# High parts of all k first, then low parts, in the weight-stationary matmuls of a two-layer float32 decoder

## The chip, the cores and the metric

One core of one Trainium2 chip. The metric is the device time of one execution in microseconds (us), as the median of several runs; shorter is better.

## What is computed

A decoder of two layers on 256 tokens of 1024 features, all in float32. Layer 0 is an mLSTM mixer, layer 1 an attention whose only block is the causal one of 256 tokens (so its block selection has no effect); each is followed by a ConvFFN. The keys and values of layer 1 are made from the residual stream after layer 0.

```
for l in range(2):
    h = h + mixer_l(rmsnorm(h))             # projections of 1024 features, w_out or w_o at the end
    u = rmsnorm(h) @ w_up                   # 1024 -> 2 x 2816
    c = conv_b + causal convolution of u over 3 tokens, by feature
    val, gate = split(c)
    h = h + (silu(gate) * val) @ w_down     # 2816 -> 1024
```

## The kernel before

**Precision.** TensorE multiplies in float32r. Each float32 operand is split into a high part (rounded to float32r) and a low part (the rest), and a product is summed from three passes: high by high, high by low and low by high. ScalarE (ACT) makes the high part of a weight unit and VectorE (DVE) the low part (`unit`, L163, the copies at L171 and L172, in two pieces). An activation is split in the same way (`split`, L175), in the ConvFFN by ACT (L339) and POOL (L340).

**Two ways of multiplying.** Most matmuls hold the weights still: a tile of 128 output features by 256 tokens is summed in one PSUM bank over all k, where k counts blocks of 128 input features. For each k, `steps_w` (L226) issues two matmuls: the high weights against the high and low parts of the activation side by side (512 columns, L241), and the low weights against the high part (256 columns, L245). The high weights times the low activation thus gather in the second half of the bank; `whole` (L278) or `residual` (L288) adds the halves. Where `apart` is false (the last tile of the kernel alone), both products of the high weights go to the first half, as two matmuls of 256 columns (L239). The v, o, and attention projections hold the activation still instead (`steps_x`, L254, three matmuls of 512 columns per k at L262 to L264).

**The order before.** The high matmul goes first for k = 0, as it opens the bank. For every later k the low one goes first, then the high one. So a tile of eight k runs high, low, low, high, low, high, and so on, and where one tile follows another, two highs meet.

**Stages.** Keys and queries of the mLSTM (`kq_steps`, eight column tiles, the first two mixed k by k with the gates' matmuls), v and o, the output projection `project_out` (L297: four column tiles over k = 0 to 3, the same four over k = 4 to 7, then four more), the up projection of the ConvFFN (`pair`, L353: 22 pairs of tiles, value and gate, the first `AHEAD` = 2 pairs k by k as the operands come), the convolution of each pair (`conv`, L319, `finish`, L333), and the down projection (`down`, L372: eight column tiles over 22 k, with two weight units of 11 k each). Down's first steps go: k = 0 to 18 of tile 0, k = 0 to 10 of tile 1, then the rest of both, so that the last convolutions have time to end. The attention layer then runs in the same pattern.

The first `DEFER` = 3 pairs of an up stage multiply an operand that lacks 1/rms; `rescale` (L342) makes the operands once more with 1/rms in them (L348 on DVE, L350 on ACT, L351 on POOL), and the pairs from 3 on use these. 1/rms comes from `Rstd` (L206): `sums` (two small matmuls at L212, then L214 on DVE and a power on POOL at L216) and `row` (transposes at L221, a copy at L223).

**What sets the order of work.** TensorE runs in the order in which the program emits its instructions. `mix` (L68) emits a list of steps, each with an assumed cost in us, and slips in other items once the summed cost reaches an item's time; a step costs 0.32. The instructions of DVE, ACT and POOL are ordered by the framework, with a simulated timeline of the program. SyncE issues the loads. Weight units pass through three raw buffers and four buffers each for the high and the low parts; five PSUM banks hold the tiles (`acc`), three more serve the rest (`mis`).

Of the kernel before, what the change touches and what calls it, by code (L numbers as in the profile page):

```python
# [42 lines left out]
# columns of the per-partition parameter array  # L43
# [5 lines left out]
# columns of the array that is needed first: the gates' weights, the first gain  # L49
# [6 lines left out]
class Once:  # L56
    """A thing that is made when it is first asked for."""
# [10 lines left out]
def mix(steps, items=()):  # L68
    """Emit the steps, each a (cost, function), and the items, each a (time, function), among them."""
    items, now = list(items), 0.0  # L70
    for cost, step in steps:
        while items and items[0][0] <= now:
            items.pop(0)[1]()
        step()
        now += cost
    for _, item in items:
        item()
# [3 lines left out]
def yoco_kernel(ctx: ExitStack, tc: tile.TileContext, A, out):  # L81
    nc = tc.nc
    # the tensor engine works in the order of this program
# [10 lines left out]
    # ---- the residual stream, transposed: hT[:, k] holds features k*128.. by tokens  # L94
# [3 lines left out]
    # rows on every partition: the gates' biases, the gains of k's and q's first 32 features  # L98
# [19 lines left out]
    # the gates' weights: for each k the high parts, the low parts, and zeros  # L118
# [3 lines left out]
    # while the first loads run: the tensor engine's clock rises, the activation tables are loaded  # L122
# [8 lines left out]
    # ---- constants made on the chip  # L131
    ident = const.tile([P, P], F32, name="ident")
    make_identity(nc, ident)
    # adds rows m and m + 8
    both8 = const.tile([4 * MH, 2 * MH], F32, name="both8")
    nc.gpsimd.tensor_tensor(out=both8, in0=ident[:4 * MH, :2 * MH], in1=ident[:4 * MH, 2 * MH:4 * MH], op=OP.add)
    # sel[:, h] has ones in row h alone
# [4 lines left out]
    # [s, t], 1 where s <= t, else 0; columns 128.. are ones  # L142
# [4 lines left out]
    # mLSTM: [s, t], 0 where s <= t, else BIG; columns 128.. are free  # L147
# [6 lines left out]
    # attention: [t, s], columns 128.. 0 where s <= t, else -BIG; the columns before are free  # L154
# [7 lines left out]
    # ---- weights: a unit is loaded whole and split exactly into two float32r parts  # L162
# [20 lines left out]
    # ---- RMSNorm: the gain goes into the matmul's operand, 1/rms is applied to its result  # L183
    # an operand: for each k its high part, its low part, and both side by side
# [21 lines left out]
    class Rstd:  # L206
        """1/rms of the residual stream: a column over the tokens and a row on every partition."""
# [17 lines left out]
    # ---- matmuls: three exact passes of hi and lo parts  # L225
    def steps_w(ps, w, at, x, ks, kall, done=None, apart=True):  # L226
        """ps[n, tokens] += W[k, n].T x[k, tokens]; at(k) gives the columns of k in w. The high parts of W
        times the low parts of x may be summed apart, in the second half of ps."""
        xh, xl, both = x

        def one(k):
            (hi, lo), p = w(), ps()
            c = slice(at(k), at(k) + P)
            last = k == kall - 1

            def high():
                if not apart:
                    for n, xs in enumerate((xh, xl)):
                        nc.tensor.matmul(p[:, :S], hi[:, c], xs[k], start=k == 0 and n == 0, stop=last and n == 1)  # L239
                    return  # L240
                nc.tensor.matmul(p, hi[:, c], both[k], start=k == 0, stop=last)  # L241

            if k == 0:
                high()
            nc.tensor.matmul(p[:, :S], lo[:, c], xh[k], start=False, stop=False)  # L245
            if k > 0:
                high()
            if last and done is not None:
                done(p)

        return [(0.32, lambda k=k: one(k)) for k in ks]

    def steps_x(t, units, x, done):
        """ps[tokens, 512] = x[k, tokens].T W[k, 512] over two units of four k."""  # L254
# [15 lines left out]
    def block_x(src, first, x, done):  # L270
        """Both token tiles of 512 columns: units first and first + 1 of src."""
# [522 lines left out]
```

## Time and profile before

| | |
|---|---|
| median of three runs | 608.62 us (608.0 to 608.84) |
| profiled execution: span from first to last instruction | 607.1 us |
| TensorE matmul busy | 593.5 us |
| TensorE weight loads busy | 505.9 us |
| VectorE busy | 495.6 us |
| ScalarE (ACT) busy | 393.2 us |
| POOL busy | 171.8 us |

The profile gives only the span of its own execution; the median of the runs lies 1.5 us above it. Busy times of different engines overlap. Matmul records overlap as well, since a matmul's record goes on after the next has started, so the distance from start to start tells the rate. A few matmul records are missing. In the trace `xa` and `xb` are two sets of projection operands, `f` is the activation of a ConvFFN, `hi` and `lo` the parts of the weights, `acc` a PSUM bank of a tile and `mis` one of the other banks.

### The profile page before, as it was taken

The numbers are of one execution on the slowest core, as the hardware profiler recorded it, in microseconds if no ns is written. First come the engines' busy times: TensorE is split into PE (matmuls) and PEld (weight loads), VectorE is DVE, ScalarE is ACT, GpSimd is POOL, SyncE is SP. The second block draws the span as 40 slices with busy tenths as digits, with TensorE's granted clock in tenths as the row PEclk, the third lists the DMA queues.
The fourth block names the chain that finished last, engine by engine and source line by source line (L and its number), as shares of the span: only waits on it lengthen the run. The fifth ranks groups of instructions, "written<-read, shape, count | busy, mean of one in ns | idle before, by whom it ended". The sixth has DMA issues, their size and how long they took to land.

```text
span 607.1 us, 8990 instructions
## 1 busy us (share of the span) xinstructions
PE 593.5 (98%) x3278; PEld 505.9 (83%) x3278; DVE 495.6 (82%) x837; ACT 393.2 (65%) x713; POOL 171.8 (28%) x186
## 2 busy tenths in 40 slices
PE   7899999999999999899999999999999999998997
PEld 4787888888888888788888878888888888887887
DVE  7897667989999999967768786467999999998550
ACT  5756776667886777755556687554878767675330
POOL 6600310352545344211111100022445453441000
PEclk8999999999999999899999999999999999999999
DMA  6874333526444543465754533335353445336530
GB/s 243 317 264 169 139 138 140 208 84 263 159 179 166 191 165 133 161 207 184 266 203 181 198 123 143 125 135 208 132 215 140 185 172 198 138 131 229 212 108 18
DMA packets 18621, 105.79 MB, mean 174 GB/s; under 512 B 2320, under 2 KB 3856, under 8 KB 9104
## 3 DMA queue, kind: packets, MB, share of 16 engines
q1 hardware_dynamic: 18576, 105.21, 47.0%
q8 instruction: 26, 0.43, 0.3%
q14 instruction: 19, 0.16, 0.1%
HBM read 104.15 MB, written 1.05 MB: 173 GB/s over the span
## 4 chain that ended last, share of the span: by engine, by line
PE 48%; DVE 37%; issue 8%; ACT 3%; POOL 2%; DMA 1%; SPq 0%; POOLq 0%; DVEq 0%; ACTq 0%
PE acc L241 15%; DVE y L329 15%; DVE lo L172 14%; PE acc L245 8%; PE acc L262 6%; PE acc L264 6%; PE acc L263 6%; DVE whole L282 4%; DVE xs L348 1%; ACT y L326 1%; DVE xa L181 1%; PE acc L239 1%; ACT hi L171 1%; DMA hT<-xT 1%; PE mis L547 1%
## 5 line engine op out<-in xcount | busy, mean ns | idle before, releaser
L172 DVE TENSOR_TENSOR lo<-raw,hi 128x1024 fp32r<-128x1024 f32 (+2 forms) x218 | 248.6, 1168 | 30.5 <-ACT hi L171 30.2
L241 PE MATMUL acc<-xb,hi 128*128 128x512 f32 x736 | 252.3, 396 | 0.6 <-POOL xb L351 0.6
L171 ACT ACTIVATE hi<-raw 128x1024 fp32r<-128x1024 f32 (+2 forms) x218 | 199.9, 964 | 61.3 <-PE acc L241 29.5
L245 PE MATMUL acc<-xb,lo 128*128 128x256 f32 x736 | 191.2, 279 | 0.0
L241 PEld LDWEIGHTS acc<-xb,hi 128*128 128x128 f32 x736 | 131.8, 188 | 26.3 <-POOL xb L351 1.3
L245 PEld LDWEIGHTS acc<-xb,lo 128*128 128x128 f32 x736 | 138.7, 188 | 8.0
L241 PE MATMUL acc<-f,hi 128*128 128x512 f32 x330 | 116.6, 398 | 1.0 <-POOL f L340 1.0
L329 DVE SCALAR_TENSOR_TENSOR y<-whole,par,y 128x254 f32<-128x254 f32 (+1 forms) x176 | 110.0, 644 | 3.2 <-ACT y L326 2.8
L245 PE MATMUL acc<-f,lo 128*128 128x256 f32 x352 | 97.5, 284 | 3.0 <-ACT f L339 3.0
L338 POOL TENSOR_TENSOR a<-sg,y 128x256 f32<-128x256 f32 x44 | 57.8, 1314 | 98.4 <-ACT sg L336 98.4
L241 PEld LDWEIGHTS acc<-f,hi 128*128 128x128 f32 x330 | 61.8, 190 | 14.5 <-POOL f L340 1.4
L245 PEld LDWEIGHTS acc<-f,lo 128*128 128x128 f32 x352 | 66.8, 190 | 5.0 <-ACT f L339 3.6
L326 ACT ACTIVATE y<-whole,par 128x256 f32<-128x256 f32 x88 | 51.7, 594 | 20.8 <-DVE whole L282 18.8
L241 PE MATMUL acc<-xa,hi 128*128 128x512 f32 x160 | 57.5, 401 | 0.7 <-DVE hT L291 0.5
L262 PE MATMUL acc<-hi,xa 128*128 128x512 f32 x128 | 53.4, 417 | 0.0
L340 POOL TENSOR_TENSOR f<-a,f 128x256 fp32r<-128x256 f32 x44 | 42.3, 962 | 36.6 <-ACT f L339 36.6
L264 PE MATMUL acc<-hi,xa 128*128 128x512 f32 x128 | 50.1, 391 | 0.0
L199 POOL TENSOR_TENSOR sqacc<-sqacc,sq 128x256 f32<-128x256 f32 x18 | 16.3, 908 | 119.0 <-ACT sq L198 119.0
L263 PE MATMUL acc<-lo,xa 128*128 128x512 f32 x128 | 50.0, 391 | 0.0
L245 PE MATMUL acc<-xa,lo 128*128 128x256 f32 x160 | 44.4, 289 | 0.8 <-DVE lo L172 0.7
L282 DVE TENSOR_TENSOR whole<-acc,whole 128x256 f32<-128x256 f32 (+1 forms) x97 | 39.4, 412 | 0.0
L281 ACT ACTIVATE whole<-acc 128x256 f32<-128x256 f32 (+1 forms) x97 | 35.4, 368 | 6.0 <-PE acc L241 5.8
(180 smaller groups left out, 637.7 us busy)
## 6 DMA issues: line engine op xcount, KB each, us to landing
raw<-w_up SPq DMA_DIRECT2D x44, 1024.0 KB, 4.8
raw<-w_down SPq DMA_DIRECT2D x32, 704.0 KB, 4.0
raw<-w_kqv SPq DMA_DIRECT2D x12, 1024.0 KB, 4.8
raw<-w_vo SPq DMA_DIRECT2D x8, 1024.0 KB, 4.8
raw<-w_out SPq DMA_DIRECT2D x4, 1024.0 KB, 4.8
raw<-w_o SPq DMA_DIRECT2D x4, 1024.0 KB, 4.8
raw<-w_kq SPq DMA_DIRECT2D x2, 1024.0 KB, 7.8
raw<-w_kq SPq DMA_DIRECT2D x4, 256.0 KB, 5.5
```

What stands on the lines that cost most here:

```text
L171: nc.scalar.activation(hi[:, c], raw[:, c], AF.Copy)
L172: nc.vector.tensor_tensor(lo[:, c], raw[:, c], hi[:, c].bitcast(F32), OP.subtract)
L241: nc.tensor.matmul(p, hi[:, c], both[k], start=k == 0, stop=last)
L245: nc.tensor.matmul(p[:, :S], lo[:, c], xh[k], start=False, stop=False)
L262: nc.tensor.matmul(p, xh[k][:, ts], hi[:, c], start=k == 0, stop=False)
L263: nc.tensor.matmul(p, xh[k][:, ts], lo[:, c], start=False, stop=False)
L264: nc.tensor.matmul(p, xl[k][:, ts], hi[:, c], start=False, stop=k == KD - 1)
L282: nc.vector.tensor_tensor(y, ps[:rows, :S], y, OP.add)
L326: nc.scalar.activation(y, u, AF.Identity, bias=b, scale=w[2])
L329: nc.vector.scalar_tensor_tensor(y[:, d:], u[:, :S - d], w[j], y[:, d:], op0=OP.mult, op1=OP.add)
L338: nc.gpsimd.tensor_tensor(out=a, in0=sg, in1=y[0], op=OP.mult)
L340: nc.gpsimd.tensor_tensor(out=al[i], in0=a, in1=ah[i].bitcast(F32), op=OP.subtract)
```

## The change

`steps_w` no longer issues one step per k with two matmuls. It returns all high matmuls of the k that it is given (0.22 us each), and then all low ones (0.11 us each). The first high still opens the bank; the last low now closes it and calls `done`. Callers that passed all k of a tile get high times eight, then low times eight. `down` calls it once per weight unit, so 11 highs are followed by 11 lows. Callers that pass one k at a time (the first two pairs of an up stage, the first two tiles of keys and queries) get high, then low, for each k. `kq_steps` takes the k as an argument for that. Comments and docstrings are taken out as well.

```diff
     def steps_w(ps, w, at, x, ks, kall, done=None, apart=True):
...
         xh, xl, both = x
 
-        def one(k):
-            (hi, lo), p = w(), ps()
+        ks = list(ks)
+
+        def high(k):
+            (hi, _), p = w(), ps()
             c = slice(at(k), at(k) + P)
+            if apart:
+                nc.tensor.matmul(p, hi[:, c], both[k], start=k == 0, stop=False)
+            else:
+                for n, xs in enumerate((xh, xl)):
+                    nc.tensor.matmul(p[:, :S], hi[:, c], xs[k], start=k == 0 and n == 0, stop=False)
+
+        def low(k):
+            (_, lo), p = w(), ps()
             last = k == kall - 1
-
-            def high():
-                if not apart:
-                    for n, xs in enumerate((xh, xl)):
-                        nc.tensor.matmul(p[:, :S], hi[:, c], xs[k], start=k == 0 and n == 0, stop=last and n == 1)
-                    return
-                nc.tensor.matmul(p, hi[:, c], both[k], start=k == 0, stop=last)
-
-            if k == 0:
-                high()
-            nc.tensor.matmul(p[:, :S], lo[:, c], xh[k], start=False, stop=False)
-            if k > 0:
-                high()
+            nc.tensor.matmul(p[:, :S], lo[:, at(k):at(k) + P], xh[k], start=False, stop=last)
             if last and done is not None:
                 done(p)
 
-        return [(0.32, lambda k=k: one(k)) for k in ks]
+        return [(0.22, lambda k=k: high(k)) for k in ks] + [(0.11, lambda k=k: low(k)) for k in ks]
...
             def down(n, ks):
                 apart = gains is not None or n < KD - 1
-                return [s for k in ks for s in
-                        steps_w(pd[n], wd[2 * n + k // 11], lambda q: (q % 11) * P, act, [k], KF,
+                return [s for u in range(2) for s in
+                        steps_w(pd[n], wd[2 * n + u], lambda q: (q % 11) * P, act,
+                                [k for k in ks if k // 11 == u], KF,
                                 lambda p: residual(n, p, gains, apart), apart)]
...
-        def kq_steps(j):
-            return steps_w(pk[j], wk[j // 2], lambda k: k * 256 + (j % 2) * P, setA, range(KD), KD,
+        def kq_steps(j, ks=range(KD)):
+            return steps_w(pk[j], wk[j // 2], lambda k: k * 256 + (j % 2) * P, setA, ks, KD,
                            (lambda p: kq_done(j)) if j > 2 else None)
...
-        s0, s1 = kq_steps(0), kq_steps(1)
-        mix([s for k in range(KD) for s in (sg[k], s0[k], s1[k])])
+        mix([s for k in range(KD) for s in [sg[k]] + kq_steps(0, [k]) + kq_steps(1, [k])])
```

## Rows read from the trace of the kernel before

**Rows 1.** The page's line of engines: busy us, share of the span, instructions.

```profile
PE 593.5 (98%) x3278; PEld 505.9 (83%) x3278; DVE 495.6 (82%) x837; ACT 393.2 (65%) x713; POOL 171.8 (28%) x186
```

**Rows 2.** Chain of waits by line: 262 to 305, 17 to 37, 150 to 262 us.

```profile
by line: PE acc L241 66.1%; PE acc L245 34.1%
...
by line: PE acc L241 38.4%; PE acc L245 19.8%; POOL tab L607 17.8%; POOL sq L394 8.2%; POOL tab L603 5.1%; issue 3.6%; POOL rc L216 3.4%; PE mis L221 2.2%; PE mis L437 1.1%; PE mis L438 1.1%; PE mis L436 0.6%
...
by line: DVE y L329 37.0%; DVE lo L172 26.3%; issue 14.8%; DVE whole L282 8.3%; PE acc L241 4.7%; ACT y L326 2.7%; PE acc L245 2.0%; ACT hi L171 1.5%; ACT sg L336 1.1%; POOL f L340 0.7%; POOL a L338 0.7%; ACT whole L281 0.5%; ACTq L336 0.0%
```

**Rows 3.** A stretch of up: busy us (xinstructions) of PE, PEld, DVE, ACT, POOL; clock.

```profile
150.00:190.00 40.00, 40.00 (x231) 34.81 (x230) 40.00 (x61) 30.90 (x62) 21.24 (x17) 1.00 0.43 169
```

**Rows 4.** The low matmuls of L245 in a stretch of down: matmuls, then weight loads.

```profile
262.00:302.00 40.00, 31.40 (x115) 21.42 (x114) 1.00 0.59 209
```

**Rows 5.** Timeline (start us, us, group): a 512-column run (35 steps), a 256-column run (42).

```profile
313.98 0.39 PE L262 MATMUL acc<-hi,xa 128*128 128x512 f32 x1
...
321.91 0.39 PE L264 MATMUL acc<-hi,xa 128*128 128x512 f32 x1
...
597.99 0.40 PE L239 MATMUL acc<-f,hi 128*128 128x256 f32 x2
...
603.03 0.40 PE L239 MATMUL acc<-f,hi 128*128 128x256 f32 x2
```

**Rows 6.** Timeline where two tiles of up meet (x2 merges two matmuls).

```profile
151.31 0.63 PE L241 MATMUL acc<-xb,hi 128*128 128x512 f32 x2
151.78 0.39 PE L245 MATMUL acc<-xb,lo 128*128 128x256 f32 x2
152.01 0.40 PE L241 MATMUL acc<-xb,hi 128*128 128x512 f32 x1
```

**Rows 7.** Timeline of layer 0 from the first down matmul to the last activation.

```profile
241.04 0.39 PE L241 MATMUL acc<-f,hi 128*128 128x512 f32 x1
...
248.34 0.41 DVE L282 TENSOR_TENSOR whole<-acc,whole 128x256 f32<-128x256 f32 x1
...
251.73 2.22 DVE L172 TENSOR_TENSOR lo<-raw,hi 128x704 fp32r<-128x704 f32 x2
...
252.00 0.39 PE L241 MATMUL acc<-f,hi 128*128 128x512 f32 x1
...
253.70 0.39 PE L245 MATMUL acc<-f,lo 128*128 128x256 f32 x1 [1.31 <-ACT f L339]
...
254.59 0.80 PE L241 MATMUL acc<-f,hi 128*128 128x512 f32 x1 [0.50 <-POOL f L340]
```

**Rows 8.** The same two waits in layer 1.

```profile
552.10 0.38 PE L245 MATMUL acc<-f,lo 128*128 128x256 f32 x1 [1.67 <-ACT f L339]
...
552.98 0.50 PE L241 MATMUL acc<-f,hi 128*128 128x512 f32 x1 [0.51 <-POOL f L340]
```

**Rows 9.** Stretches right behind these waits, columns as in rows 3 (clock: third last).

```profile
254.30:257.80 3.50, 3.21 (x10) 2.73 (x11) 3.30 (x6) 2.96 (x6) 0.23 (x1) 0.52 0.69 232
...
554.40:557.80 3.40, 3.40 (x21) 3.01 (x20) 2.77 (x5) 1.02 (x2) 0.00 (x0) 1.00 0.94 331
```

**Rows 10.** Timeline of the first up tile with rescaled operands: first high, eighth high.

```profile
134.19 0.40 PE L241 MATMUL acc<-xb,hi 128*128 128x512 f32 x1
...
137.21 0.73 PE L241 MATMUL acc<-xb,hi 128*128 128x512 f32 x2 [0.32 <-POOL xb L351]
```

**Rows 11.** Timeline of keys and queries: the power on POOL, the row's transposes.

```profile
23.64 0.71 POOL L216 TENSOR_TENSOR rc<-ms,mhalf 128x2 f32<-128x2 f32 x1
...
24.41 0.43 PE L221 MATMUL mis<-ident,rc 128*128 128x128 f32 x2 [0.63 <-POOL rc L216]
```

**Rows 12.** Timeline of the first output projection: last operand, its high matmul.

```profile
99.89 0.48 DVE L181 SCALAR_TENSOR_TENSOR xb<-mis,par,xb 128x256 fp32r<-128x256 f32 x1 [0.54 <-ACT xb L180]
...
100.42 0.50 PE L241 MATMUL acc<-xb,hi 128*128 128x512 f32 x1
```

**Rows 13.** Timeline of VectorE: its first rescaled operands in layer 0.

```profile
125.38 0.88 DVE L348 SCALAR_TENSOR_TENSOR xs<-hT,par,rB 128x256 f32<-128x256 f32 x2 [2.33 <-ACT rB L223]
```

## The prediction

> **What bounds the kernel now.** I read the page's engine line first, then the chain of waits by stretch, then start times of single matmuls. TensorE is busy for nearly the whole span [rows 1], but matmul records overlap, so that alone proves nothing. The chain, cut by stretch, does [rows 2]. From 262 to 305 us (down projection of layer 0) it consists of TensorE's own matmuls and nothing else. From 17 to 37 us (keys and queries) it is TensorE, after a piece on POOL. From 150 to 262 us (up projection and the start of down) it is VectorE: the convolution, the low parts of the weights, the sums of the halves; TensorE has 7%. VectorE is there 40.00 of 40 us busy [rows 3]; TensorE never waits either, it only runs ahead. The proof comes at the end: the last up matmul is followed by the first down one at 241.0 us, while VectorE forms the sum of the last up tile at 248.34 us [rows 7], and TensorE then waits for the last activation. So a faster or slower TensorE matters in the down stages, in keys and queries and in the two output projections; in the up stages it mostly changes the wait that follows them.
>
> Counting tiles times k in the code: the up stages have 2 x 22 x 2 x 8 = 704 pairs of a high (512 columns) and a low matmul (256). On TensorE's path are 3 x 64 = 192 pairs outside the ConvFFN and 330 in down (the last tile's 22 steps have three matmuls of 256 and stay as they are in cost); 64 of these run before the wait for the last activation and are covered. That leaves about 460 pairs.
>
> **Rate of the matmuls.** The edit adds and removes no matmul, load or byte on TensorE; it changes which size follows which. A pair takes 40.00/114 = 351 ns in down [rows 4]; I use 350. Grouped runs of 8 or 11 are not in the trace, so I bound them from the nearest rows. A long run of 512 columns with new weights each time takes (321.91 - 313.98)/35 = 227 ns, and a long run of 256 columns (603.03 - 597.99)/42 = 120 ns [rows 5]; both together 347, or 3 ns less per pair. Where two tiles meet, the present order already has two highs and then two lows in a row: 0.47/2 = 235 and 0.23/2 = 115 ns, in sum 350 [rows 6]. The best mixture, 227 + 115, is 8 ns less, the worst, 235 + 120, 5 ns more: -3.7 to +2.3 us over 460 pairs. The new runs begin like the border and go on like the long runs, so I take the middle of the two observed sums, -2 ns a pair: **-0.9 us**.
>
> The trace shows no waiting of a low matmul on its weights: lows in a run keep 115 to 120 ns. The Trainium skill (TensorE: Matmul & The Clock Gate, section Back-to-back issue gap) gives a warm matmul its columns over 2.4 GHz plus 2.5 ns whatever precedes it, thus 325 ns for a pair in either order, by which this term would be nil; the rows show 25 ns more than that, and in both kinds of run, so the measurement decides.
>
> **Wait for the last activation, twice.** Now down runs 19 k of column tile 0, 11 k of tile 1, then k = 19 to 21 of tile 0, alternating. The high of k = 20 goes at 252.00, the low of 21 waits until 253.70 for the high part of the activation, the high of 21 until 254.59 for the low part that POOL makes [rows 7]; layer 1 does the same at 552.10 and 552.98 [rows 8]. After the change the three highs come first, and the high of 21 needs both parts. It still starts at about 254.6, as its operand comes from VectorE and POOL, but the lows of 19, 20 and 21 (3 x 0.12 us) then stand behind it instead of ahead: 0.35 us per layer, **+0.7 us**. Ends: 0, if the activation arrives as early as TensorE does; +0.7.
>
> That wait has a second price. Behind it in layer 0 the granted clock falls: 10 matmuls in 3.5 us at 0.52, where layer 1 after its wait has 21 in 3.4 us at 1.00 [rows 9]. Half of 3.4 us, 1.7 us, is lost once in this execution. Whether it is lost again depends on the idle time of TensorE there, which two shifts change. Two lows fewer go before it (0.24 us more idle). And TensorE arrives later: at the first tile with rescaled operands its highs start at 134.19, and the eighth waits until 137.21 for POOL's last low part [rows 10]; in the new order the tile's eight lows (8 x 0.12 us), which now go ahead of that high, stand behind the wait, and the tile ends 0.9 us later. VectorE's lag covers those 0.9 us; without that lag they would be +0.9 us a layer. The idle time goes from about 2.1 us in two parts to 2.6 - 0.9 = 1.7 us in one. Layer 1's 1.67 + 0.51 us [rows 8] cost no clock, so I can't tell from the length alone. I keep one such stretch, as now: **0**, ends -1.7 and +1.7 us.
>
> **Keys and queries.** The row of 1/rms waits at 24.41 for POOL, whose turn at 23.64 comes behind its table work [rows 11]; nothing that TensorE does moves that. Now 12 pairs stand ahead of it. With the new costs (0.22 per high, 0.11 per low) it comes after 8 pairs and the 4 highs of the next tile. Four lows move behind the wait: **+0.5 us** (ends 0 and +0.5). That the first highs no longer wait for VectorE's low weights is worth nothing: the same POOL wait takes it.
>
> **Output projections.** The last operand of the first one is ready at 100.37 (99.89 + 0.48), its high goes at 100.42 [rows 12]. In the new order it is due four lows earlier, less one low by which the transposes before it are emitted earlier: a wait of about 0.35 us, in part taken in by VectorE, which sets the chain soon after. **+0.2 us** (ends 0 and +0.35). In the second one the operands are ready over 1 us ahead: nil.
>
> **Edits at nothing.** The sums and the row of an up stage are emitted up to one pair earlier; VectorE idles 2.33 us before the row's first use [rows 13], so it could start 0.1 us earlier, and the high ahead of the low in the first, single-k steps needs VectorE's operand 0.12 us earlier: these cancel (ends -0.4 and +0.4). SyncE's loads keep their order. A unit's high buffer comes free up to 0.9 us earlier than now, its low buffer 0.1 us later; ACT waits for the former, VectorE's work is not reduced. The docstrings and comments cost nothing.
>
> **Sum.** -0.9 + 0.7 + 0 + 0.5 + 0.2 = +0.5 us on a span of 607.1 us. The page gives no other time of that execution; the median of the runs, 608.62 us, lies 1.5 us above its span, which I keep: **609.1 us**. About 0.2% (1.2 us) is what a measurement of this kernel tells from no change: 607.4 to 609.8 us is "same".
>
> **Rivals.**
> - The clock falls in layer 1 as well. Place: the one wait ahead of the high of k = 21; it decides once the idle time there, now unbroken, counts as layer 0's does. For it: layer 0 already pays with a like wait. Against: layer 1 didn't, and the wait gets shorter by the later arrival. Price +1.7 us: 610.8 us, slower.
> - The clock falls in neither, as TensorE arrives 0.9 us later and idles less. For it: 1.7 against 2.1 us. Against: that is one unbroken stretch. 609.1 - 1.7 = 607.4 us, at the bound of faster.
> - The excess over the columns belongs to the change of size, and grouped runs go at the best of both rows (342 ns a pair). 460 x 8 ns = 3.7 instead of 0.9 us: 606.3 us. Against: both long runs have excess of their own. The rule of the Trainium skill named above has no excess of this size, which speaks for it.
> - The queues of VectorE, ACT and POOL are ordered by a simulated timeline, which sees another TensorE order. Ahead of the last activation stand two low parts of down weights (2.22 us for a pair [rows 7]); one unit more or fewer there moves the end of an up stage by that much: 607 or 611.3 us.
>
> **How the numbers follow.** Forecast with one stretch of low clock: 0.40, its own range 607.8 to 610.4. Clock falls twice 0.18, never 0.18, best rows 0.10, rearranged queues 0.14. Faster by over 0.2%: best rows, half of "never", half of the rearranged ones, a small tail of the forecast, 0.28. Slower: clock twice, half of the rearranged ones, the forecast's tail, 0.34. Same: 0.38. The range that leaves out 2 in 10 reaches from the best rows to a second clock fall with a slower rate: 605.6 to 611.8 us.
>
> **What would show it.** Right: pairs in down (high and low starts counted over 40 us) at 345 to 352 ns; the high of k = 21 still near the same distance from VectorE's last sums, with three lows behind it; TensorE's wait for the eighth rescaled operand longer by 0.9 us; the row at 24.4 us as now. Wrong: pairs under 343 or over 355 ns; an end of the up stages that moves with TensorE instead of VectorE; the number of half-clock stretches other than one.

## The result, and the profile after

The changed kernel takes **615.06 us** (median of 13 runs, 610.23 to 617.44) against 608.84 us (13 runs, 607.46 to 610.64): a ratio of 1.0086 with a 95% interval of 1.0068 to 1.0103. It is slower by more than the 0.2% that can be told apart, and above the whole predicted range. The profiled execution took 616.29 us, with a span of 614.6 us against 607.1 us before.

The runs differ among themselves more than before, and with the granted clock. The two with a mean clock of 0.999 and 1.0 took 610.23 and 610.27 us; the two slowest, 617.44 and 616.48 us, have 0.981 and 0.983. So most of the loss is not in the order of the matmuls as such.

The page of the kernel after: the engine line, the granted clock in 40 slices, the chain by engine.

```profile
PE 599.0 (97%) x3278; PEld 512.5 (83%) x3278; DVE 478.1 (78%) x837; ACT 392.5 (64%) x713; POOL 173.1 (28%) x186
...
PEclk9699999999999999999999999999999999998999
...
PE 56%; DVE 18%; ACT 9%; issue 7%; POOL 7%; DMA 1%; SPq 0%; POOLq 0%; DVEq 0%; ACTq 0%
```

The counts of instructions are those of [rows 1]. The new thing is the 6 in the second slice of the clock (15 to 31 us), and an 8 in the fourth slice from the end. Three stretches are at half clock (the one at 259.5 us lies across two slices and shows in no digit), here by the view of windows (engines in the order PE, PEld, DVE, ACT, POOL; then clock, DMA share, GB/s):

```profile
20.50:30.80 10.30, 10.24 (x36) 8.82 (x37) 8.66 (x14) 5.14 (x9) 3.73 (x6) 0.50 0.72 259
259.50:262.90 3.40, 3.20 (x9) 2.72 (x10) 3.40 (x6) 2.23 (x4) 0.14 (x1) 0.50 0.82 244
559.90:563.30 3.40, 3.40 (x10) 2.66 (x9) 2.36 (x5) 0.60 (x1) 0.00 (x0) 0.50 0.94 318
```

TensorE ran at 1.2 GHz (clock 0.50) for 10.3 us in keys and queries, and for 3.4 us in each of the two down stages. In the profile before, the first of these windows has this row:

```profile
20.50:30.80 10.30, 9.67 (x58) 8.36 (x59) 8.14 (x17) 7.16 (x12) 3.86 (x6) 1.00 0.73 278
```

58 matmuls instead of 36, at full clock. Of the other two, layer 0's was there before and layer 1's was not [rows 9].

Where the 7.5 us between the two spans lie, as lengths of stages in us, each worked out from the start of its first matmul to the start of the next stage's (the last row: to the start of its own last matmul):

| stage | before | after | after - before |
|---|---|---|---|
| keys and queries from the sums on, to v and o | 17.70 | 21.84 | +4.14 |
| v and o | 54.56 | 54.55 | 0.0 |
| output projection, layer 0 | 23.47 | 23.75 | +0.28 |
| up, layer 0 | 124.85 | 124.85 | 0.0 |
| down, layer 0 | 65.43 | 66.53 | +1.10 |
| attention with its output projection | 107.68 | 107.51 | -0.17 |
| up, layer 1 | 124.92 | 124.74 | -0.18 |
| down, layer 1 | 64.44 | 66.65 | +2.21 |

Before the sums, 0.1 us comes on top. So three places matter, keys and queries and the two down stages, and in each of them TensorE waits. The list of TensorE's waits after shows them at its head, both down stages in one line (us in total, times, longest):

```profile
PE acc L237 <- POOL f L338: 6.0, 2, 3.0
PE mis L212 <- DVE sqacc L395: 2.4, 1, 2.4
```

**Keys and queries.** TensorE's timeline of the kernel after (start, duration, group; in brackets the idle time before it and what ended it):

```profile
16.10 2.03 PE L237 MATMUL acc<-xa,hi 128*128 128x512 f32 x8
20.56 0.98 PE L212 MATMUL mis<-tri,sqacc 128*128 128x1 f32 x4 [2.44 <-DVE sqacc L395]
21.41 2.05 PE L245 MATMUL acc<-xa,lo 128*128 128x256 f32 x8
23.26 1.91 PE L237 MATMUL acc<-xa,hi 128*128 128x512 f32 x4
...
26.05 0.69 PE L221 MATMUL mis<-ident,rc 128*128 128x128 f32 x2
```

and of the kernel before, the two waits in the same place:

```profile
18.71 0.39 PE L245 MATMUL acc<-xa,lo 128*128 128x256 f32 x1 [0.43 <-DVE lo L172]
...
20.46 0.58 PE L212 MATMUL mis<-tri,sqacc 128*128 128x1 f32 x4 [0.78 <-DVE sqacc L396]
```

The sums start at the same time, 20.46 and 20.56, since they hang on VectorE. Before, a low matmul stopped at 18.71 for its weights, and matmuls went on from there to the next wait. After, the eight highs need no low weights, run through by 18.1, and TensorE then stands still in one piece of 2.44 us. Behind that piece the clock is at half: the first eight lows take until 23.26, which is (23.26 - 21.41)/8 = 231 ns each, twice the 115 ns of [rows 6].

The idle time is not only in one piece, it is also longer: 2.44 us against 0.43 + 0.78 us. Eight highs (8 x 0.233 us) stand ahead of the sums where six pairs did (6 x 0.35 us), and TensorE came to them 0.6 us earlier in this execution. No run here changes the one and keeps the other.

**Start of down.** The last k of tile 0, layer 0 and then layer 1, on TensorE and POOL after:

```profile
245.56 0.87 PE L237 MATMUL acc<-f,hi 128*128 128x512 f32 x3
...
256.10 0.63 PE L237 MATMUL acc<-f,hi 128*128 128x512 f32 x2
258.84 0.80 POOL L338 TENSOR_TENSOR f<-a,f 128x256 fp32r<-128x256 f32 x1 [0.53 <-ACT f L337]
259.70 0.79 PE L237 MATMUL acc<-f,hi 128*128 128x512 f32 x1 [2.97 <-POOL f L338]
260.29 0.84 PE L245 MATMUL acc<-f,lo 128*128 128x256 f32 x3
...
558.50 0.50 PE L237 MATMUL acc<-f,hi 128*128 128x512 f32 x1 [2.99 <-POOL f L338]
558.83 0.51 PE L245 MATMUL acc<-f,lo 128*128 128x256 f32 x3
```

The two waits of [rows 7] and [rows 8] (1.31 + 0.50 and 1.67 + 0.51 us) are one of 2.97 or 2.99 us, and three lows stand behind it. The last activation has landed when POOL has made its low part; the high of k = 21 follows 0.05 us later. From the first high of down to this landing it is 258.84 + 0.80 - 245.56 = 14.08 us after, and was 13.50 us before. In layer 1 the same distance is 13.86 us before and 14.10 us after. Why it is later in layer 0 stands in VectorE's timeline after:

```profile
252.62 2.23 DVE L172 TENSOR_TENSOR lo<-raw,hi 128x704 fp32r<-128x704 f32 x2
254.77 0.41 DVE L280 TENSOR_TENSOR whole<-acc,whole 128x256 f32<-128x256 f32 x1
```

The last up tile's halves are summed 9.21 us into down, behind a pair of low parts (the two pieces of one unit of down's weights). Before, the sum came at 7.30 us into down and the low parts after it [rows 7]. The order of VectorE's queue is another one.

**Rate.** In down after, (2.73 - 0.40)/10 = 233 ns for a high in a run of eleven and (1.46 - 0.28)/10 = 118 ns for a low, in sum 351 ns, from these rows:

```profile
252.23 2.73 PE L237 MATMUL acc<-f,hi 128*128 128x512 f32 x11
254.80 1.46 PE L245 MATMUL acc<-f,lo 128*128 128x256 f32 x11
```

Alternating it was 351 ns [rows 4].

### The profile page after: what moved, and what is told of

The parts are those of the page before. It is cut to its first block, busy times and chain, and to the rows that moved or that the text cites. A ratio compares the mean times of both kernels' runs of the same rounds, so it can differ in the third digit from the quotient of the medians.

```text
span 614.6 us, 9033 instructions
## 1 busy us (share of the span) xinstructions
PE 599.0 (97%) x3278; PEld 512.5 (83%) x3278; DVE 478.1 (78%) x837; ACT 392.5 (64%) x713; POOL 173.1 (28%) x186
## 4 chain that ended last, share of the span: by engine, by line
PE 56%; DVE 18%; ACT 9%; issue 7%; POOL 7%; DMA 1%; SPq 0%; POOLq 0%; DVEq 0%; ACTq 0%
PE acc L237 20%; PE acc L245 11%; DVE y L327 8%; DVE lo L172 7%; PE acc L260 6%; PE acc L262 6%; PE acc L261 6%; POOL a L336 5%; ACT hi L171 4%; ACT y L324 3%; DVE whole L280 2%; POOL xb L349 2%; ACT sg L334 1%; ACT whole L279 1%; DMA hT<-xT 1%
## 5 line engine op out<-in xcount | busy, mean ns | idle before, releaser
L172 DVE TENSOR_TENSOR lo<-raw,hi 128x1024 fp32r<-128x1024 f32 (+2 forms) x218 | 242.8, 1139 | 29.4 <-ACT hi L171 28.8
L237 PE MATMUL acc<-xb,hi 128*128 128x512 f32 x736 | 187.6, 393 | 1.0 <-POOL xb L349 0.6
L245 PEld LDWEIGHTS acc<-xb,lo 128*128 128x128 f32 x736 | 101.5, 190 | 7.7
L327 DVE SCALAR_TENSOR_TENSOR y<-whole,par,y 128x255 f32<-128x255 f32 (+1 forms) x176 | 93.1, 565 | 18.7 <-ACT y L324 17.7
L245 PE MATMUL acc<-xb,lo 128*128 128x256 f32 x736 | 104.2, 282 | 0.0
L237 PE MATMUL acc<-f,hi 128*128 128x512 f32 x330 | 85.3, 405 | 6.0 <-POOL f L338 6.0
L237 PE MATMUL acc<-xa,hi 128*128 128x512 f32 x160 | 52.7, 418 | 0.2
L245 PEld LDWEIGHTS acc<-f,lo 128*128 128x128 f32 x352 | 46.8, 190 | 2.9
L245 PE MATMUL acc<-f,lo 128*128 128x256 f32 x352 | 47.6, 282 | 0.0
L337 ACT ACTIVATE f<-a 128x256 fp32r<-128x256 f32 x44 | 18.3, 416 | 40.8 <-POOL a L336 40.6
```

The source lines that it names most:

```text
L172: nc.vector.tensor_tensor(lo[:, c], raw[:, c], hi[:, c].bitcast(F32), OP.subtract)
L237: nc.tensor.matmul(p, hi[:, c], both[k], start=k == 0, stop=False)
L245: nc.tensor.matmul(p[:, :S], lo[:, at(k):at(k) + P], xh[k], start=False, stop=last)
L327: nc.vector.scalar_tensor_tensor(y[:, d:], u[:, :S - d], w[j], y[:, d:], op0=OP.mult, op1=OP.add)
```

## The experiments

**The theory**, A in the expectations: grouping gathers TensorE's waits into unbroken ones, the clock falls behind them, and some low matmuls go behind the wait instead of ahead. **The rivals**: the other engines' queues, reordered by the simulated timeline, bring the operands later; or grouped matmuls, or the lows at the end of a tile, cost time in themselves. Where an expectation gives a theory another letter or another price, its own words say so. All times are medians, ratios are to the kernel before in the same session, with 95% intervals. No kernel leaves out any part of the computation.

### One caller put back at a time

A flag `alt` in `steps_w` brings back the alternating order for one caller, all else as after. The sketch is the same for four kernels:

```diff
-    def steps_w(ps, w, at, x, ks, kall, done=None, apart=True):
+    def steps_w(ps, w, at, x, ks, kall, done=None, apart=True, alt=False):
...
+        if alt:
+            return [(0.32, lambda k=k: one(k)) for k in ks]
         return [(0.22, lambda k=k: high(k)) for k in ks] + [(0.11, lambda k=k: low(k)) for k in ks]
```

**Keys and queries put back**

```diff
         def kq_steps(j, ks=range(KD)):
...
-                           (lambda p: kq_done(j)) if j > 2 else None)
+                           (lambda p: kq_done(j)) if j > 2 else None, alt=True)
```

> The changed kernel with keys and queries back in the old, alternating order; all else as changed. Theory A (the loss is idle time of TensorE that the new order gathers into unbroken waits, and the clock that falls behind them): the unbroken 2.4 us wait ahead of the sums is split again, the 10 us at half clock behind it goes, the v/o stage starts near 38.2 us as before and not at 42.4, and the time falls by about 4 us to 611 (ratio to the kernel before 1.003 to 1.005). Theory B (the grouped runs themselves, or the other engines' queue orders in the up stages, cost the time): a twentieth of the pairs is changed, so the time stays at 614 to 615 (1.008 to 1.010).

Measured: 612.25 us (610.44 to 614.76), 1.0056 [1.0035, 1.0077]. It gives back 2.8 of the 6.2 us, not the 4 that theory A expected, and lies between the two forecasts. From the sums to v and o it takes 18.55 us instead of 21.84. The waits are broken up again, though the clock still falls once, for 3.4 us (timeline of this kernel, then the window):

```profile
18.46 0.38 PE L246 MATMUL acc<-xa,lo 128*128 128x256 f32 x1 [0.85 <-DVE lo L172]
...
20.20 0.58 PE L212 MATMUL mis<-tri,sqacc 128*128 128x1 f32 x4 [0.79 <-DVE sqacc L411]
```

```profile
20.80:24.20 3.40, 3.40 (x12) 2.90 (x12) 2.02 (x4) 2.04 (x3) 3.30 (x6) 0.50 0.71 253
```

So a broken wait here is no safeguard. Nor does its shorter stretch at half clock show that breaking up helps: the next kernel has 3.4 us too, behind a wait of 2.29 us in one piece. The same profile prices the clock in down: in layer 1 the clock did not fall, with the same distance to the landing and a wait as long and as unbroken as the 2.99 us of the kernel after, and the stage took 65.07 instead of 66.65 us. One fall costs 1.6 us there.

```profile
554.89 0.50 PE L237 MATMUL acc<-f,hi 128*128 128x512 f32 x1 [2.97 <-POOL f L354]
```

**Down put back**

```diff
-                                lambda p: residual(n, p, gains, apart), apart)]
+                                lambda p: residual(n, p, gains, apart), apart, alt=True)]
```

> The changed kernel with the down projections back in the old order. Theory A: the wait for the last activation is broken up by a low matmul again and the three lows go ahead of it; the down stages take 65.4 and 64.4 us as before (66.5 and 66.7 in the changed kernel), in sum 3 us less, time about 612 (1.005 to 1.007). If the later last activation (0.6 us) comes from the other engines' queue order in the up stages, 0.6 us per layer of it stays. Theory B: the down stages hold a quarter of the pairs; 613.5 to 615.

Measured: 612.62 us (610.64 to 613.0), 1.0058 [1.0038, 1.0077]. Down takes 66.01 us with a fall in layer 0 and 64.66 without one in layer 1. The activation still lands 14.11 us after down's start: its delay doesn't come from down's order. From the sums to v and o this execution took 18.81 us, with a fall of 3.4 us, although keys and queries are grouped here as in the kernel after. The length of that fall is not fixed by the order there.

**Both put back**

> Keys and queries and the down projections in the old order; the high-first runs are left in the up projections and the two output projections, which hold 832 of the 1248 pairs. Theory A: as the kernel before within 1 us, 608.5 to 610 (0.999 to 1.002). Theory B: most of the loss stays, 612 to 614 (1.005 to 1.009).

The edit is both of the above. Measured: 610.33 us (608.29 to 613.95, 12 runs), 1.0038 [1.0018, 1.0058], a little over what was expected. The clock falls in both places of the profile (18.57 us from the sums on; down 66.16 and 64.66 us), and the landing is still at 14.11 us. What is left grouped, up and the output projections, therefore has a cost of its own, the later landing.

**Up and the output projections put back**, the rest grouped

```diff
-                           lambda p: residual(n, p, gains))
+                           lambda p: residual(n, p, gains), alt=True)
...
-                        for s in steps_w(ps[i][half], w[i], lambda k, half=half: k * 256 + half * P, x, ks, KD)]
+                        for s in steps_w(ps[i][half], w[i], lambda k, half=half: k * 256 + half * P, x, ks, KD, alt=True)]
```

> The reverse: up projections and output projections in the old order, high-first runs in keys and queries and in down alone. Theory A: as the changed kernel, 614 to 616 (1.007 to 1.011). Theory B: near the kernel before, 609 to 611.5 (1.001 to 1.005).

Measured: 612.58 us (612.04 to 614.31), 1.0067 [1.0049, 1.0085]: 2.5 us less than after, where a theory of the two other places alone leaves little to gain. It lies between the two forecasts, and neither was met. The landing is back at 13.56 and 13.50 us. In layer 1 the clock doesn't fall (down 64.49 us), in layer 0 it does (66.10 us); from the sums on it is 20.87 us, with 6.8 us at half clock. The rival of the reordered queues is right about the landing: the order of the matmuls in these two stages sets it (which of the two, the kernel with up alone grouped tells below).

### The waits filled

If it is the clock, matmuls that do nothing useful should remove the loss without moving any operand. `fill` multiplies the tile `warm`, which the start-up already uses, into a bank that nobody reads:

```diff
+    def fill(n):
+        ps = mis()
+        for _ in range(n):
+            nc.tensor.matmul(ps, warm[:, :P], warm, start=True, stop=True)
```

**Keys and queries filled**, the kernel after with ten of these ahead of the sums

```diff
-            [(1.5, r.sums), (3.2, gates), (3.2, row_done), (9.6, sums_f), (14.0, maxima)])
+            [(1.5, lambda: (fill(10), r.sums())), (3.2, gates), (3.2, row_done), (9.6, sums_f), (14.0, maxima)])
```

> The changed kernel with ten matmuls of zeros (512 columns, bf16, their result unused) ahead of the sums in keys and queries, to fill TensorE's 2.4 us wait; no work is taken away. Theory A (the clock that falls behind the unbroken wait makes the loss there): no fall of the clock between 20 and 31 us, the v/o stage starts at 37.5 to 38.5 us instead of 42.4 (3.4 to 10 us at half clock cost 0.6 to 4 us in the runs so far), time 611 to 612.5, a mean clock above that of the changed kernel's runs. Theory B (the wait itself, or the lows behind it, make the loss): TensorE has more to do and the time stays at 615 or rises.

Measured: 612.26 us (610.72 to 613.67, 11 runs), 1.0048 [1.0029, 1.0067]. The window that had 36 matmuls at half clock:

```profile
20.50:30.80 10.30, 10.30 (x62) 8.66 (x61) 8.76 (x16) 7.43 (x12) 3.63 (x6) 1.00 0.75 280
```

Now 62 at full clock, and v and o start at 38.40 instead of 42.40 us (38.16 before). In down both falls are there as in the kernel after (66.41 and 66.61 us).

**Down filled**, the kernel after with twelve ahead of the high of k = 21

```diff
-            mix(down(0, range(19)) + down(1, range(11)) + down(0, range(19, KF)) + down(1, range(11, KF)))
+            rest = down(0, range(19, KF))
+            mix(down(0, range(19)) + down(1, range(11)) + rest[:2] + [(0.0, lambda: fill(12))] + rest[2:]
+                + down(1, range(11, KF)))
```

> The changed kernel with twelve such matmuls ahead of the high matmul of k = 21, in the 3 us wait for the last activation of each up stage. Theory A: the clock no longer falls after that wait in either layer; the down stages take 65 us each (66.5 and 66.7 in the changed kernel), time about 612. Theory B: no gain, as the activation still lands 14.1 us into the stage: 615.

Measured: 611.97 us (610.0 to 613.11, 12 runs), 1.0047 [1.0031, 1.0064]. No fall in down, 65.17 and 65.07 us instead of 66.53 and 66.65. In keys and queries TensorE came later in this execution and waited 1.28 us for the sums; behind that wait the clock stayed full. POOL's power for 1/rms then took 1.69 us instead of 0.71 [rows 11], so that TensorE waited a second time, and there the clock fell for 3.4 us (timeline, then the window):

```profile
25.25 0.43 PE L221 MATMUL mis<-ident,rc 128*128 128x128 f32 x2 [1.83 <-POOL rc L216]
```

```profile
26.40:29.80 3.40, 3.40 (x13) 3.03 (x13) 3.40 (x7) 2.96 (x5) 0.00 (x0) 0.50 0.66 253
```

**Both filled**

> Both fillings in the changed kernel. Theory A: hardly any stretch at half clock is left after the start, the mean clock is 0.996 or more, and the time comes to 609 to 611, with less spread; what is left above the kernel before is the later activation (0.6 and 0.2 us) and the lows behind the two waits (0.4 to 0.5 us each). Theory B: 615 or more.

Measured: 609.43 us (609.29 to 609.56, 12 runs), 1.0005 [0.9989, 1.0021]. After the start-up the clock doesn't fall, and the spread of the runs is 0.3 us instead of 7.2. The two gains add: 615.06 - 612.26 = 2.8 and 615.06 - 611.97 = 3.1 give 5.9, and both together give 5.6 us. TensorE's timeline of this kernel, in keys and queries and at the start of down, layer 0:

```profile
16.47 2.02 PE L237 MATMUL acc<-xa,hi 128*128 128x512 f32 x8
18.33 2.33 PE L289 MATMUL mis<-warm 128*128 128x512 bf16 x10
20.50 0.52 PE L212 MATMUL mis<-tri,sqacc 128*128 128x1 f32 x4
...
24.39 0.43 PE L221 MATMUL mis<-ident,rc 128*128 128x128 f32 x2 [0.85 <-POOL rc L216]
...
252.66 2.77 PE L289 MATMUL mis<-warm 128*128 128x512 bf16 x12
255.80 0.50 PE L237 MATMUL acc<-f,hi 128*128 128x512 f32 x1 [0.36 <-POOL f L343]
256.13 0.52 PE L245 MATMUL acc<-f,lo 128*128 128x256 f32 x3
```

The operands come when they came without filling (the sums at 20.50; the landing 14.09 us into down); only the clock is another. The wait for POOL's 1/rms, which the prediction built on, is visible again at 24.39: in the kernel after, half a clock had made TensorE too late to meet it.

**The kernel before, filled** in the same places: four ahead of the sums, six and two around the last low of k = 21, where its two waits are

```diff
+            if pre[0]:
+                fill(pre[0])
             nc.tensor.matmul(p[:, :S], lo[:, c], xh[k], start=False, stop=False)
+            if pre[1]:
+                fill(pre[1])
...
-            mix(down(0, range(19)) + down(1, range(11)) + down(0, range(19, KF)) + down(1, range(11, KF)))
+            mix(down(0, range(19)) + down(1, range(11)) + down(0, range(19, KF), (6, 2)) + down(1, range(11, KF)))
...
-            [(1.5, r.sums), (3.2, gates), (3.2, row_done), (9.6, sums_f), (14.0, maxima)])
+            [(1.5, lambda: (fill(4), r.sums())), (3.2, gates), (3.2, row_done), (9.6, sums_f), (14.0, maxima)])
```

> The kernel before with filling: four matmuls of zeros ahead of the sums, six and two around the last low matmul of the last activation's k. If the falls of the clock are what idle time costs there as well, the fall after layer 0's wait goes (1.6 us) and the time is 606 to 608 (0.996 to 0.999), below both kernels; if not, 608.6 as now or slightly more.

Measured: **607.12 us** (606.92 to 607.73, 12 runs), 0.9976 [0.9962, 0.9991], the fastest of all kernels here. The high of k = 21 goes at the same place as in [rows 7], and the clock, 0.52 in [rows 9], is now full in that window:

```profile
252.18 1.47 PE L295 MATMUL mis<-warm 128*128 128x512 bf16 x6
253.69 0.39 PE L247 MATMUL acc<-f,lo 128*128 128x256 f32 x1
253.92 0.61 PE L295 MATMUL mis<-warm 128*128 128x512 bf16 x2
254.59 0.51 PE L241 MATMUL acc<-f,hi 128*128 128x512 f32 x1
```

```profile
254.40:257.80 3.40, 3.34 (x19) 2.81 (x19) 3.37 (x6) 2.96 (x6) 0.14 (x1) 1.00 0.82 273
```

This splits the loss. Filling takes 5.6 us from the kernel after and 608.63 - 607.12 = 1.5 us from the one before. So of the 6.4 us between 615.06 and 608.63, 4.1 us are clock, and 609.43 - 607.12 = 2.3 us are something else.

### The other 2.3 us: one part grouped alone, with filling

These start from the filled kernel before (607.12 us), so that the clock is out of the way. They use the order of after for one caller and `alt` for the others; the filling stays in, with ten or twelve matmuls where the wait is in one piece. The diffs are against the kernel that has `alt` for every caller, in effect the filled kernel before. The kernel before takes 608.79 us in the session of these kernels and 608.63 in that of the filled ones. In the expectation of up alone, "from here on" means all four kernels of this section.

**Keys and queries alone**

```diff
             return steps_w(pk[j], wk[j // 2], lambda k: k * 256 + (j % 2) * P, setA, ks, KD,
-                           (lambda p: kq_done(j)) if j > 2 else None, alt=True)
+                           (lambda p: kq_done(j)) if j > 2 else None)
...
-            [(1.5, lambda: (fill(4), r.sums())), (3.2, gates), (3.2, row_done), (9.6, sums_f), (14.0, maxima)])
+            [(1.5, lambda: (fill(10), r.sums())), (3.2, gates), (3.2, row_done), (9.6, sums_f), (14.0, maxima)])
```

> High-first runs in keys and queries alone, the wait ahead of the sums filled. Theory A: four lows move behind the wait for the row of 1/rms and nothing else: the stage from the sums to v and o takes 18.1 us (17.7 in the kernel before with filling), time 607.5 to 607.7.

Measured: 607.66 us (607.4 to 608.18), 0.9975 [0.9965, 0.9985]; from the sums to v and o 18.18 us instead of 17.71. The four lows behind the wait for 1/rms cost 0.47 us, as expected.

**Down alone**

```diff
-                                lambda p: residual(n, p, gains, apart), apart, alt=True, pre=pre)]
+                                lambda p: residual(n, p, gains, apart), apart)]
...
+            rest = down(0, range(19, KF))
+            mix(down(0, range(19)) + down(1, range(11)) + rest[:2] + [(0.0, lambda: fill(12))] + rest[2:]
+                + down(1, range(11, KF)))
```

> High-first runs in the down projections alone. Theory A: the activation lands at 13.6 and 13.9 us as before, and the three lows behind it cost 0.35 us per layer, with 0 to 1.3 ns more per pair 0.1 us each: 607.8 to 608.1. Theory C: it lands at 14.1 us, 608.3 or more.

Measured: 607.80 us (607.64 to 608.04), 0.9977 [0.9967, 0.9987]. The landing stays at 13.57 and 13.58 us, and down takes 64.60 and 64.59 us. The kernel with only keys and queries grouped has the same landing to 0.1 us and down at 64.17 and 64.16 us. So grouped down costs 0.43 us a layer, near the three lows' 0.35, and doesn't move the landing.

**Up alone**

```diff
-                        for s in steps_w(ps[i][half], w[i], lambda k, half=half: k * 256 + half * P, x, ks, KD, alt=True)]
+                        for s in steps_w(ps[i][half], w[i], lambda k, half=half: k * 256 + half * P, x, ks, KD)]
```

> From here on every kernel has matmuls of zeros in the waits, so that the clock does not fall, and is read against the kernel before with filling (607.12 us). High-first runs in the up projections alone. Theory A (the late last activation comes from the order of the other engines' queues that the new up order brings): the last activation lands 14.1 us into both down stages instead of 13.6 and 13.9, down takes 0.5 and 0.1 to 0.2 us more, the up stages 0.1 to 0.2 us less, time 607.3 to 607.9. Theory C (it comes from the order in down): landing as in the kernel before, time 607.0.

Measured: 608.83 us (608.54 to 609.17, 11 runs), 0.9995 [0.9982, 1.0009], 0.9 us over the upper end of the expectation. The landing is at 14.13 and 14.12 us, so the mechanism holds: POOL's last low part, and with it the high of k = 21, comes later though down itself is alternating. Up alone, then down alone, on POOL and TensorE, layer 0; down's first high is at 241.21 and at 240.90:

```profile
241.21 0.39 PE L237 MATMUL acc<-f,hi 128*128 128x512 f32 x1
...
254.54 0.81 POOL L363 TENSOR_TENSOR f<-a,f 128x256 fp32r<-128x256 f32 x1 [0.53 <-ACT f L362]
255.40 0.50 PE L237 MATMUL acc<-f,hi 128*128 128x512 f32 x1
```

```profile
240.90 1.79 PE L237 MATMUL acc<-f,hi 128*128 128x512 f32 x7
...
253.66 0.81 POOL L359 TENSOR_TENSOR f<-a,f 128x256 fp32r<-128x256 f32 x1 [0.53 <-ACT f L358]
254.52 0.51 PE L237 MATMUL acc<-f,hi 128*128 128x512 f32 x1
```

Down takes 64.70 us in both layers. But the up stages are longer, 125.15 and 125.22 us against 124.88 and 124.93 of the filled kernel before. In the kernel with all callers grouped and filled the up stages take 124.75 us. The extra time lies ahead of the first tile with rescaled operands, which in layer 0 starts 18.36 us into up, against 17.97 us with all callers grouped; from there to down both take 106.8 us. What makes it later was not tried. The spans of the two profiled executions differ by 1.2 us, and the stages account for that. The other 0.5 us of the medians' 1.7 is in the execution that was profiled of the filled kernel before: at 607.57 us it is one of four of its twelve runs above 607.5, where the other eight are at 607.16 or less.

**The tail alone put back**, the kernel after, both filled, with k = 19 to 21 of tile 0 alternating

```diff
-            rest = down(0, range(19, KF))
-            mix(down(0, range(19)) + down(1, range(11)) + rest[:2] + [(0.0, lambda: fill(12))] + rest[2:]
-                + down(1, range(11, KF)))
+            mix(down(0, range(19)) + down(1, range(11)) + down(0, range(19, KF), True, (9, 2)) + down(1, range(11, KF)))
```

> The changed kernel with filling (609.43 us), but k = 19 to 21 of the first down tile alternate again, so that the three lows go ahead of the last wait. Theory A: 0.35 us per layer less, 608.6 to 608.9, with the activation still landing at 14.1 us. If the lows behind the wait cost nothing: 609.4.

Measured: 608.76 us (608.44 to 609.13), 0.9998 [0.9982, 1.0014]; 0.67 us less than with both filled. Down takes 64.79 and 64.75 us instead of 65.09 twice, with the landing at 14.14 and 14.12 us as before: 0.3 us a layer are the three lows behind the wait, and none of it is the rate of the rest of down.

## Why the prediction was wrong

**Keys and queries, the step that failed.** It said that the first highs no longer waiting for VectorE's low weights "is worth nothing: the same POOL wait takes it". The time of the operands was right. But with that wait gone TensorE stands still at the sums for 2.44 us in one piece, where it had 0.43 + 0.78 us, and 10.2 us of half clock follow in the profiled run: 21.84 us where the two filled kernels with the same order take 18.11 and 18.18, thus 3.7 us for the clock alone. So the failed step is a cost put at nothing: the prediction weighed the clock at the start of down and didn't look for the same effect here, where the clock before is full. Its own sign of being wrong, a number of half-clock stretches other than one, came: there are three. That the fall comes behind the wait, and that filling the wait removes it, is shown; whether the length or the single piece brings it is not. The rest of the step was right: the four lows behind the wait for 1/rms were put at +0.5 and measured 0.47 us.

**Wait for the last activation, mis-sized.** The kept case was one fall of the clock in one of the two layers; the profiled run has two. The rival "the clock falls in layer 1 as well" described this and put 1.7 us on it; 1.4 to 1.6 us were measured (66.53 and 66.65 against 65.09 us filled). The length of the wait went wrong by two terms. "2.6 - 0.9 = 1.7 us in one" took 0.9 us for TensorE's later arrival from the first rescaled tile. That tile's highs start at 138.78 and the next tile at 142.21, so it takes 3.43 us, against 137.55 - 134.19 = 3.36 before (137.55 is the second of the two highs merged in [rows 10]): 0.1, not 0.9, and the up stage is as long as it was.

```profile
138.78 1.86 PE L237 MATMUL acc<-xb,hi 128*128 128x512 f32 x7
140.92 0.50 PE L237 MATMUL acc<-xb,hi 128*128 128x512 f32 x1 [0.28 <-POOL xb L349]
142.21 1.09 PE L237 MATMUL acc<-xb,hi 128*128 128x512 f32 x4
```

The eighth high, which was to wait 0.9 us longer, waits as long as before (0.28 and 0.32 us), since POOL's operand is there earlier: that high goes 20.21 us into up, before 21.02. The prediction had these operands come as before, with ends of 0.4 us either way. And the activation lands 0.6 us later in layer 0, 0.2 in layer 1. The starting value is loose as well: the brackets of [rows 7] give 1.81 us of idle time, the starts 2.24, the prediction says about 2.1. With 2.6 + 0.6 = 3.2 us in place of 1.7, the estimate is near the 2.97 us measured. The three lows behind the wait, +0.35 a layer, measured 0.3 to 0.43 us.

**Rearranged queues.** This rival, at 0.14, had the right row: VectorE's pair of low parts, 2.2 us, now goes ahead of the last sum instead of behind it. Of the 2.2 us only 0.6 arrive at the landing. The runs show that the order of the matmuls in up brings it about: with up alone grouped the last sum comes 9.25 us into down, with down alone grouped 7.37. That the simulated timeline does this was not shown, only that the queue differs; a fixed order wasn't tried.

**Rate of the matmuls.** -0.9 us was wrong in sign and small: from start to start, pairs take 349.2 ns in up (349.6 before) and 351.5 in down (350.3 before, though 351.1 in every other kernel here with an alternating down), 0.1 to 0.3 us over all. The middle of the two observed sums was the wrong choice; the border of two tiles [rows 6] was the better row, as it had both sizes in the new order. The Trainium skill (TensorE: Matmul & The Clock Gate, section Back-to-back issue gap) makes the gap a matter of the columns alone in the formula that the prediction used, which the section gives for an isolated matmul; for a stream of weight loads and matmuls, as here, the same section gives about 131 ns at 512 columns. The trace agrees that the order hardly matters, and with neither figure: a high takes 233 ns, a pair 351 and not 325.

**Output projections.** In layer 0, +0.2 us was put and +0.28 measured; in layer 1, nil was put and +0.03 measured. The wait that was forecast in layer 0 is there after (0.24 us for `xb`):

```profile
103.42 0.87 PE L237 MATMUL acc<-xb,hi 128*128 128x512 f32 x3
104.53 0.50 PE L237 MATMUL acc<-xb,hi 128*128 128x512 f32 x1 [0.24 <-DVE xb L181]
```

**The sum.** The terms without the clock make +0.7 + 0.5 + 0.2 = 1.4 us with no gain in rate; 1.7 us lie between the spans of the two filled kernels (607.6 and 605.9), 2.3 between their medians (the profiled execution of the filled kernel before is 0.45 us above its median). That part was right in kind; it lacks the later landing, which the prediction took as fixed: 14.09 us against 13.56 in layer 0. The clock was the part that decided, and it was put at 0 with ends of 1.7 us either way, where the medians show 4.1 us.

**What stays open**: why the fall in keys and queries lasts 3.4 us in some executions, 6.8 or 10.2 in others, and what the two runs at 610.2 us did there, whose mean clock of 0.999 and 1.0 leaves room for hardly any fall; whether the longer wait or the single piece makes the falls more frequent; and why the rescaled operands come later in the kernel with up alone grouped.

## What to carry to other kernels

A reordering that takes away a small wait ahead of a larger one can cost more than it saves: look how long the engine then stands still, and what the granted clock does behind such pieces elsewhere in the same trace. Where TensorE has a wait that nothing can remove, a few idle matmuls in it are nearly free and keep the clock up; here that made the kernel before 0.24% faster and its runs agree to 0.8 us instead of 5.4 us (of the same session). And when one engine's order changes under a scheduler that simulates a timeline, compare the order of the others before pricing anything.

## What the runs showed of the hardware that was not expected

The same program can lose very different amounts behind the same wait: the runs of the kernel after go from 610.23 us at a mean clock of 0.999 to 617.44 us at 0.981. The stretches at half clock that were seen in keys and queries lasted 3.4, 6.8 and 10.2 us. A wait of 2.99 us in one piece at the start of down, layer 1, was followed by 3.4 us at half clock (the kernel after), one of 2.97 us at the same place by none (keys and queries put back). One of 0.85 us with another of 0.79 us behind it and some matmuls between was followed by 3.4 us at half clock (keys and queries put back), while 1.67 and 0.51 us [rows 8] cost nothing. In the kernel with down filled, the clock stayed full behind a wait of 1.28 us and fell behind a second one of 1.83 us. So the length of one wait doesn't tell whether the clock falls, and neither does its being in one piece.
